# Stored gate vectors as 32 rows, a last norm of two operations per half, and a residual rebuilt by the next block

## The chip, the cores and the metric

The kernel runs on one core of a Trainium2 chip. The engines of the core are named as in the profile: PE (TensorE, matmuls) with its weight loads as PEld, DVE (VectorE), ACT (ScalarE), POOL (GpSimd) and SP (SyncE, which issues most transfers). The metric is the device time of one execution in microseconds; the time given is the median of several runs. An engine works through its own instructions in the order in which they were written to it, and waits on semaphores for what the others have to deliver.

## The reference

Two layers, each of three blocks: a feed-forward network, a mixer, a feed-forward network. Activations are 512 tokens of 1,024 float32 values. A conditioning vector gives shift, scale and gate for each block.

```
mod = (silu(c) @ ada_w[l] + ada_b[l]).reshape(Bn, N_SUB, 3, D_MODEL)
shift, scale, gate = mod[:, :, 0, None], mod[:, :, 1, None], mod[:, :, 2, None]
h = x * (1.0 + scale[:, 0]) + shift[:, 0]
y = swiglu(h, ffn_w1[l, 0], ffn_w3[l, 0], ffn_w2[l, 0])
x = layer_norm(ALPHA * x + 0.5 * (1.0 + gate[:, 0]) * y, ln_g[l, 0], ln_b[l, 0])
```

`swiglu(h, w1, w3, w2)` is `(silu(h @ w1) * (h @ w3)) @ w2` with an inner width of 2,816. The second block has `hybrid_mixer` (attention, spatial gating and a state-space scan over one input and one output projection) in place of `swiglu` and a weight of 1 in place of 0.5, and the third is like the first. The result is x after the third block of the second layer.

## The kernel before

All float32 matmuls are three matmuls of a reduced format, on a high and a low part of each operand (`mm3`, L121 to L123). Weights come in tiles of 128x1024 (512 KB) by SP's queue into four buffers `raw`; `wsplit` has ACT make the high part (L103) and DVE the low part (L105). `wsplit_s` does so in halves, named wsh and wsl (L116, L117), for the last four tiles of w2 in an FFN.

**An FFN** (`ffn`) first projects two lead tiles of the inner width (four in the first block), then the others one by one: tiles h of w1 and w3 over 1,024 inputs, `swiglu`, and the result split into `ghi` and `glo`. After each half of the 22 tiles come the down matmuls y. The gate is no operation on y: `down_weights` multiplies each w2 tile by the row G on DVE (L101, L111) before it is split. In the second half the last four w2 tiles are kept, and the matmuls go token block by token block (four blocks of 128 tokens, numbered 0 to 3; 24 matmuls each), so that the norm of one block runs beside the matmuls of the next.

**The norm** (`post_norm`). DVE adds y to the residual x in two halves (L242) with statistics behind each (L243), aggregates them (L256) and prepares the variance (L230); POOL raises it to the power -0.5 (L231); DVE makes the second scale factor (L258); ACT writes the normed block z (L267), not yet multiplied by ln_g and ln_b. `flush` calls `spread`: PE transposes z into PSUM (hps, L213), ACT and DVE apply the next block's scale and shift to it (hsum, L224 and L222), and it is split into `hT_hi` and `hT_lo` (L226, L227), the operands of the next block. What the next block needs of x itself, the residual, is z times ln_g plus ln_b: `renew` writes it with two 128x1024 DVE operations per token block (L279, L280), called at the end of `ffn` and of `mixer`. z, lg, lb and G share a pool of eight buffers of 128x1024 (`big`) with the background work's tiles.

In the last block there is no next one: ACT writes z in halves, DVE multiplies and adds (L263, L264), and each half is stored to the output. For token blocks 0 to 2 the statistics there are a sum taken with the addition (L239) and a sum of squares on ACT.

**The gate vectors.** `ada_vec` computes one of the 18 vectors of 1,024 values as 128x8 (value 128k+p in partition p, column k). It runs in the background of the other work, a step at a time (`make_bg`). A gate (j == 2) has to become a row that is the same in all partitions, so it is stored to DRAM by POOL's queue (L183) and read back by `gate_par` with a broadcast (L188):

```
G.dma_start(bass.AP(tensor=d.tensor, offset=d.offset, ap=[[1, 128], [128, 8]]), acc)
load(g, bcast_row(mods[l, s, 2][0], 1024))
```

**The order.** Each engine's order follows from the order in which the program is written and from a scheduler in the tile framework. `tc.issue_after(ins)` puts what is written inside it behind the instruction `ins` on that instruction's engine. The mixer begins with two groups of matmuls per token block, tA (24 of 128x284) and tB (24 of 128x256), in the same PSUM pool as part of the FFN's y; a GELU on DVE reads tB.

Five changes from one block to the next are spoken of by letters: A (first FFN to first mixer, near 380 us), B (mixer to FFN, near 680), C (FFN to the next layer's FFN, near 1,050), D (FFN to second mixer, near 1,410), E (mixer to last FFN, near 1,710). The last FFN's end is the tail.

## Time and profile before

| | us |
|---|---|
| median of 3 runs (2077.01 to 2079.93) | 2077.14 |
| the profiled execution's own time | 2078.03 |
| its span in the profile | 2076.3 |
| PE busy | 2036.6 |
| DVE busy | 1325.9 |
| ACT busy | 771.7 |
| POOL busy | 33.4 |

The mean granted clock of PE is 0.996 of full speed. The profile gives times of instructions in microseconds from the start of the span. "Busy" is time in which an engine had an instruction in work; where two overlap, it counts once. An idle time in square brackets stands before an instruction, with what ended it. "PEclk" is the granted clock of a stretch: 1.00 is the 2.4 GHz level, 0.50 the 1.2 GHz level. A transfer's landing is the time from its issue to its end.

### The profile page before, as it was taken

How to read it: one execution, taken by the hardware profiler on the slowest of the kernel's cores; microseconds unless marked ns; L12 is line 12 of the kernel's file. 1: busy time of each engine (PE TensorE's matmuls, PEld its weight loads, DVE VectorE, ACT ScalarE, POOL GpSimd, SP SyncE). 2: the span in 40 equal slices, each digit the busy share in tenths (PEclk: the TensorE clock that was granted, in tenths of full speed). 3: DMA queues.
4: the chain of work that ended last, by engine and by line, in shares of the span. 5: the costliest groups of instructions: out<-in, count | busy, mean ns of one | idle time of the engine just before them, and what ended most of it. 6: DMA issues, size and time to landing. Idle time of an engine off the chain costs nothing.

```text
span 2076.3 us, 25861 instructions
## 1 busy us (share of the span) xinstructions
PE 2036.6 (98%) x9992; PEld 1650.7 (79%) x9992; DVE 1325.9 (64%) x2423; ACT 771.7 (37%) x1350; POOL 33.4 (2%) x49
## 2 busy tenths in 40 slices
PE   7999999999999999999999999999999999999997
PEld 6888887887666988888888888888776678888886
DVE  6756437778898647444754644478788984354354
ACT  4422223525556422222442222235356573222222
POOL 0000000000000000000000000000000000000000
PEclk9999999999999999999999999999999999999999
DMA  8765425224452544432644443252254523232321
GB/s 334 258 177 209 168 88 157 91 97 166 133 164 90 183 142 151 143 123 83 177 125 132 144 152 126 86 145 102 92 173 132 171 79 128 71 122 94 99 92 41
DMA packets 84599, 282.34 MB, mean 136 GB/s; under 512 B 13267, under 2 KB 13523, under 8 KB 84476
## 3 DMA queue, kind: packets, MB, share of 16 engines
q1 hardware_dynamic: 83612, 278.02, 41.3%
q0 software_dynamic: 864, 2.67, 0.4%
q8 instruction: 78, 1.28, 0.2%
q14 instruction: 45, 0.37, 0.1%
HBM read 278.51 MB, written 4.76 MB: 136 GB/s over the span
## 4 chain that ended last, share of the span: by engine, by line
PE 88%; DVE 6%; DMA 2%; ACT 2%; issue 1%; POOL 0%; SPq 0%; POOLq 0%; ACTq 0%; DVEq 0%
PE h L121 15%; PE h L122 15%; PE h L123 15%; PE y L121 7%; PE y L123 7%; PE y L122 7%; PE pj L121 3%; PE pj L122 3%; PE pj L123 3%; PE op L925 3%; PE tp L915 2%; DMA raw<-in_w_dram 1%; PE S L884 1%; DVE wlo L105 1%; PE S L885 1%
## 5 line engine op out<-in xcount | busy, mean ns | idle before, releaser
L103 ACT CAST whi<-raw 128x1024 fp32r<-128x1024 f32 x308 | 320.5, 1047 | 748.0 <-issue 393.6
L121 PE MATMUL h<-hT_hi,whi 128*128 128x512 f32 (+1 forms) x1504 | 565.3, 377 | 12.9 <-ACT hT_hi L1059 12.9
L122 PE MATMUL h<-hT_lo,whi 128*128 128x512 f32 (+1 forms) x1504 | 565.9, 376 | 0.0
L123 PE MATMUL h<-hT_hi,wlo 128*128 128x512 f32 (+1 forms) x1504 | 565.5, 376 | 0.0
L105 DVE TENSOR_TENSOR wlo<-raw,whi 128x1024 fp32r<-128x1024 f32 x308 | 372.7, 1215 | 263.9 <-ACT whi L103 263.4
L121 PEld LDWEIGHTS h<-hT_hi,whi 128*128 128x128 f32 x1504 | 283.5, 189 | 64.3 <-ACT hT_hi L1059 12.9
L122 PEld LDWEIGHTS h<-hT_lo,whi 128*128 128x128 f32 x1504 | 283.6, 189 | 51.5 <-DVE hT_lo L1060 0.4
L123 PEld LDWEIGHTS h<-hT_hi,wlo 128*128 128x128 f32 x1504 | 283.6, 189 | 51.4
L121 PE MATMUL y<-whi,ghi 128*128 128x512 f32 x576 | 224.1, 389 | 0.0
L122 PE MATMUL y<-wlo,ghi 128*128 128x512 f32 x576 | 224.1, 389 | 0.0
L123 PE MATMUL y<-whi,glo 128*128 128x512 f32 x576 | 224.1, 389 | 0.0
L311 DVE TENSOR_TENSOR th<-th,h 128x512 f32<-128x512 f32 x88 | 60.4, 687 | 226.7 <-PE h L123 226.0
L154 DVE CUSTOM_DVE_ANT_0 raw<-raw,csil 128x1024 f32<-128x1024 f32 x144 | 174.2, 1217 | 0.9 <-DMA raw<-in_ada_w_dram 0.8
L123 PEld LDWEIGHTS y<-whi,glo 128*128 128x128 f32 x576 | 108.1, 188 | 22.5
L121 PEld LDWEIGHTS y<-whi,ghi 128*128 128x128 f32 x576 | 108.1, 188 | 22.4
L122 PEld LDWEIGHTS y<-wlo,ghi 128*128 128x128 f32 x576 | 108.1, 188 | 22.4
L121 PE MATMUL pj<-hT_hi,whi 128*128 128x512 f32 x288 | 117.4, 408 | 0.0
L122 PE MATMUL pj<-hT_lo,whi 128*128 128x512 f32 x288 | 113.7, 395 | 0.0
L123 PE MATMUL pj<-hT_hi,wlo 128*128 128x512 f32 x288 | 113.3, 393 | 0.0
L101 DVE TENSOR_TENSOR raw<-raw,G 128x1024 f32<-128x1024 f32 x86 | 104.3, 1218 | 4.0 <-DMA raw<-in_w_dram 4.0
L314 ACT CAST ghi<-th 128x512 fp32r<-128x512 f32 x88 | 54.4, 618 | 136.1 <-DVE th L311 136.1
L917 ACT COPY pt<-tp 128x512 f32<-128x512 f32 (+2 forms) x96 | 54.8, 584 | 83.9 <-PE tp L915 82.8
(284 smaller groups left out, 2528.1 us busy)
## 6 DMA issues: line engine op xcount, KB each, us to landing
raw<-in_w_dram SPq DMA_DIRECT2D x256, 512.0 KB, 3.6
raw<-in_ada_w_dram SPq DMA_DIRECT2D x144, 512.0 KB, 4.4
raw<-in_wS_dram SPq DMA_DIRECT2D x36, 512.0 KB, 3.6
raw<-in_cw_dram SPq DMA_DIRECT2D x16, 512.0 KB, 3.8
raw<-in_wo_dram SPq DMA_DIRECT2D x16, 512.0 KB, 4.5
raw<-in_wl_dram SPq DMA_DIRECT2D x8, 512.0 KB, 9.0
T<-lane SPq DMA_DIRECT2D x16, 256.0 KB, 3.7
G<-mod SPq DMA_DIRECT2D x6, 512.0 KB, 6.1
```

Of the source, the lines that this page charges most:

```text
L101: V.tensor_mul(raw, raw, gain)
L103: S.copy(hi[:, :n], raw[:, :n])
L105: V.tensor_sub(lo[:, :n], raw[:, :n], hi[:, :n].bitcast(F32))
L121: PE.matmul(o, lh, rh, start=first, stop=False)
L122: PE.matmul(o, lh, rl, start=False, stop=False)
L123: PE.matmul(o, ll, rh, start=False, stop=last)
L154: V.tensor_tensor_reduce(out=raw, in0=raw, in1=cond["c"], scale=0.5, scalar=0.0, op0=ALU.mult, op1=ALU.add, accum_out=acc[:, k:k + 1])
L311: freed[0] = V.tensor_mul(th, th, h3).ins
L314: S.copy(hi, th)
L915: PE.transpose(tp[0:n, e * 128:(e + 1) * 128], pr[e][:, kb * 128:kb * 128 + n], ident)
L917: S.copy(pt[0:n, :], tp[0:n, :])
L925: PE.matmul(op[r, :], v, pt[0:n, g * 256:(g + 1) * 256], start=(br == 0), stop=(br == 2 and kb == qb))
```

## The change

Three parts. First, the gate vector is put together in the first 8 columns of a raw buffer, DVE transposes 32x32 squares of it, and what was 128x8 becomes four groups of 8 rows of 32 values, each stored by a DMA of its own; G is read back by POOL's queue and no longer by SP's. Second, in the last block z becomes (x - mean)*ln_g, written before the power is known, and the output z*power + ln_b (`finish`); both are DVE operations, and the finish of token block 2 is held until behind the aggregation of block 3. Third, `renew` is called by the following block and stands behind the last scale factor of the norm.

```diff
-        else:
+        elif j == 1:
             V.scalar_tensor_tensor(acc, acc, 1.0, ab, op0=ALU.add, op1=ALU.add)
         mods[l, s, j] = acc
         if j == 2:
+            V.scalar_tensor_tensor(raw[:, 0:8], acc, 1.0, ab, op0=ALU.add, op1=ALU.add)
+            V.transpose(raw[:, 32:64], raw[:, 0:32])
             d = dram.tile([1, 1024], F32, tag=nm("mod"), name=nm("mod"))
-            G.dma_start(bass.AP(tensor=d.tensor, offset=d.offset, ap=[[1, 128], [128, 8]]), acc)
+            for b in range(4):
+                G.dma_start(bass.AP(tensor=d.tensor, offset=d.offset + 32 * b, ap=[[128, 8], [1, 32]]),
+                            raw[32 * b:32 * b + 8, 32:64])
             mods[l, s, j] = d
...
-        load(g, bcast_row(mods[l, s, 2][0], 1024))
+        G.dma_start(g, bcast_row(mods[l, s, 2][0], 1024))
...
+    def finish(b, mv, P):
+        for q in range(2):
+            sl = slice(q * 512, (q + 1) * 512)
+            x = x_sb[:, b, sl]
+            V.scalar_tensor_tensor(x, P["t"][b][:, sl], mv[:, 2:3], P["lb"][:, sl], op0=ALU.mult, op1=ALU.add)
+            load(out[b * 128:(b + 1) * 128, sl], x)
...
-            V.tensor_mul(mv[:, 3:4], mv[:, 0:1], mv[:, 2:3])
...
-            V.scalar_tensor_tensor(mv[:, 3:4], mv[:, 0:1], -1.0, mv[:, 2:3], op0=ALU.mult, op1=ALU.mult)
+            if not last:
+                P["moved"] = V.scalar_tensor_tensor(mv[:, 3:4], mv[:, 0:1], -1.0, mv[:, 2:3], op0=ALU.mult,
+                                                    op1=ALU.mult).ins
         if last:
+            P.setdefault("t", {})[b] = z
             for q in range(2):
                 sl = slice(q * 512, (q + 1) * 512)
-                S.activation(z[:, sl], x[:, sl], AF.Identity, bias=mv[:, 3:4], scale=mv[:, 2:3])
-                V.tensor_mul(x[:, sl], z[:, sl], P["lg"][:, sl])
-                V.tensor_add(x[:, sl], x[:, sl], P["lb"][:, sl])
-                load(out[b * 128:(b + 1) * 128, sl], x[:, sl])
+                V.scalar_tensor_tensor(z[:, sl], x[:, sl], mv[:, 0:1], P["lg"][:, sl],
+                                       op0=ALU.add if b < 3 else ALU.subtract, op1=ALU.mult)
+            if b == 2:
+                P["held"] = mv
+            elif b == 3:
+                with tc.issue_after(aggr.ins):
+                    finish(2, P["held"], P)
+                finish(b, mv, P)
+            else:
+                finish(b, mv, P)
             return
...
     def renew(P, n=0):
-        while len(P.get("zz", [])) > n:
-            x, z = P["zz"].pop(0)
-            V.tensor_mul(x, z, P["lg"])
-            V.tensor_add(x, x, P["lb"])
+        if len(P.get("zz", [])) > n:
+            with tc.issue_after(P["moved"]):
+                while len(P["zz"]) > n:
+                    x, z = P["zz"].pop(0)
+                    V.tensor_mul(x, z, P["lg"])
+                    V.tensor_add(x, x, P["lb"])
...
                 ahead = up_weights(todo[0])
+                catch_up()
...
         flush(P)
-        renew(P)
...
             V.bn_aggr(gmv[:, b * 2:b * 2 + 2], st)
+        catch_up()
...
+        catch_up = partial(renew, P)
         P = {}
```

The lines of the changed program carry other numbers: the addition is L247, the statistics L248, the aggregation L267, the preparation of the variance L235, the scale factor L270, the renewal L301 and L302, hT_lo L232, the transposes L218, and the matmuls L122 to L124.

How the order moves is shown at three places. The first is DVE at A, around the norm of token block 2 (statistics st_2698, mv_2699; the residual add of its halves reads y_2288 and y_2289). In the kernel before, renewals (L279, L280) of token block 1 stand between the additions and the aggregation:

```order
L242 TENSOR_TENSOR x_sb<-y_2288,x_sb 128x512
L279 TENSOR_TENSOR x_sb<-z_2640,lg_1093 128x1024
L227 TENSOR_TENSOR hT_lo<-hsum_2631,hT_hi 128x512
L243 BN_STATS st_2698<-x_sb 128x6
L242 TENSOR_TENSOR x_sb<-y_2289,x_sb 128x512
L280 TENSOR_TENSOR x_sb<-x_sb,lb_1094 128x1024
L243 BN_STATS st_2698<-x_sb 128x6
L227 TENSOR_TENSOR hT_lo<-hsum_2684,hT_hi 128x512
L222 TENSOR_SCALAR hsum_2691<-hps_2679,GA_1749,BB_1750 128x128
L256 BN_AGGR mv_2699<-st_2698 128x2
```

In the changed kernel the same token block (st_2706, mv_2707, y_2292 and y_2293) has no renewal there:

```order
L247 TENSOR_TENSOR x_sb<-y_2292,x_sb 128x512
L248 BN_STATS st_2706<-x_sb 128x6
L232 TENSOR_TENSOR hT_lo<-hsum_2639,hT_hi 128x512
L247 TENSOR_TENSOR x_sb<-y_2293,x_sb 128x512
L248 BN_STATS st_2706<-x_sb 128x6
L267 BN_AGGR mv_2707<-st_2706 128x2
L235 TENSOR_SCALAR mv_2707<-mv_2707 128x1
L270 SCALAR_TENSOR_TENSOR mv_2707<-mv_2707 128x1
```

All four renewals there now stand behind the last scale factor (mv_2767), among the first operations of the mixer (dtx):

```order
L270 SCALAR_TENSOR_TENSOR mv_2767<-mv_2767 128x1
L301 TENSOR_TENSOR x_sb<-z_2588,lg_1097 128x1024
L232 TENSOR_TENSOR hT_lo<-hsum_2752,hT_hi 128x512
L227 TENSOR_SCALAR hsum_2759<-hps_2747,GA_1753,BB_1754 128x128
L302 TENSOR_TENSOR x_sb<-x_sb,lb_1098 128x1024
L232 TENSOR_TENSOR hT_lo<-hsum_2759,hT_hi 128x512
L486 TENSOR_TENSOR dtx_2841<-tA_2848,p_461_2804 128x4
L301 TENSOR_TENSOR x_sb<-z_2648,lg_1097 128x1024
L301 TENSOR_TENSOR x_sb<-z_2708,lg_1097 128x1024
```

The operations are the same in number; what moved is the place of 128x1024 operations.

The second place is PE at A, from the last matmul y on. Before, nine matmuls tA stand between it and the transposes of token block 2 (z_2700):

```order
L123 MATMUL y_2291<-wsh_2547,glo_2267 128x512
L121 MATMUL tA_2848<-whi_2813,hT_hi 128x284
L122 MATMUL tA_2848<-wlo_2815,hT_hi 128x284
L123 MATMUL tA_2848<-whi_2813,hT_lo 128x284
...
L213 MATMUL hps_2734<-cst,z_2700 128x128 x4
L213 MATMUL hps_2739<-cst,z_2700 128x128 x4
```

In the changed kernel the transposes of that token block (z_2708) come directly behind the last y:

```order
L124 MATMUL y_2295<-wsh_2555,glo_2271 128x512
L218 MATMUL hps_2742<-cst,z_2708 128x128 x4
L218 MATMUL hps_2747<-cst,z_2708 128x128 x4
L122 MATMUL tA_2848<-whi_2813,hT_hi 128x284
L123 MATMUL tA_2848<-wlo_2815,hT_hi 128x284
```

The nine tA matmuls moved behind them; the transposes of token block 3 (z_2768) follow after 30 matmuls tA and tB.

The third place is DVE in the tail (st_16471 and mv_16472 are those of token block 3, z_16431 is block 2's). Before:

```order
L263 TENSOR_TENSOR x_sb<-z_16431,lg_14300 128x512
L242 TENSOR_TENSOR x_sb<-y_16080,x_sb 128x512
L264 TENSOR_TENSOR x_sb<-x_sb,lb_14301 128x512
L263 TENSOR_TENSOR x_sb<-z_16431,lg_14300 128x512
L243 BN_STATS st_16471<-x_sb 128x6
L264 TENSOR_TENSOR x_sb<-x_sb,lb_14301 128x512
L256 BN_AGGR mv_16472<-st_16471 128x2
```

Now (st_16482, mv_16483 and z_16484 are block 3's, z_16449 is block 2's):

```order
L247 TENSOR_TENSOR x_sb<-y_16104,x_sb 128x512
L248 BN_STATS st_16482<-x_sb 128x6
L267 BN_AGGR mv_16483<-st_16482 128x2
L254 SCALAR_TENSOR_TENSOR x_sb<-z_16449,mv_16448,lb_14325 128x512
L235 TENSOR_SCALAR mv_16483<-mv_16483 128x1
L276 SCALAR_TENSOR_TENSOR z_16484<-x_sb,mv_16483,lg_14324 128x512 x2
L254 SCALAR_TENSOR_TENSOR x_sb<-z_16449,mv_16448,lb_14325 128x512
L254 SCALAR_TENSOR_TENSOR x_sb<-z_16484,mv_16483,lb_14325 128x512 x2
```

Block 2's last operations moved behind the aggregation of block 3, and ACT has none of it.

## Rows read from the trace of the kernel before

**Rows 1.** The page's first part: busy time of each engine, its share of the span, and its instructions.

```profile
PE 2036.6 (98%) x9992; PEld 1650.7 (79%) x9992; DVE 1325.9 (64%) x2423; ACT 771.7 (37%) x1350; POOL 33.4 (2%) x49
```

**Rows 2.** The table of waits over the whole span, two of PE's: what waited, for what, us in total, times, the longest.

```profile
PE h L121 <- ACT hT_hi L1059: 12.9, 1, 12.9
...
PE hps L213 <- ACT z L267: 6.3, 5, 2.1
```

**Rows 3.** Busy time by stretch: the stretch in us and its length, then busy time (and instructions) of PE, PEld, DVE, ACT and POOL, the granted clock PEclk, the busy share of the DMA engines, and GB/s.

```profile
340.00:400.00 60.00, 55.55 (x288) 47.64 (x287) 43.69 (x73) 30.75 (x66) 2.83 (x5) 0.94 0.47 122
362.76:366.16 3.40, 3.40 (x9) 2.67 (x9) 3.33 (x5) 0.00 (x0) 0.00 (x0) 0.50 0.86 282
386.65:390.05 3.40, 3.40 (x17) 3.40 (x16) 2.50 (x6) 3.40 (x9) 0.55 (x1) 0.50 0.02 5
660.00:690.00 30.00, 28.75 (x188) 23.60 (x187) 25.77 (x51) 21.49 (x48) 2.55 (x2) 1.00 0.36 118
1015.00:1060.00 45.00, 43.32 (x267) 38.51 (x266) 34.04 (x55) 24.28 (x47) 2.21 (x4) 1.00 0.47 158
1380.00:1430.00 50.00, 47.85 (x292) 42.60 (x291) 37.16 (x68) 27.70 (x65) 2.81 (x5) 1.00 0.34 111
2060.00:2077.00 17.00, 3.69 (x17) 2.72 (x15) 9.91 (x22) 4.28 (x6) 1.10 (x2) 0.68 0.25 93
```

**Rows 4.** The same view, same columns, before and during a store of a gate vector (first two), and during and behind another (last two).

```profile
334.00:338.00 4.00, 4.00 (x19) 3.34 (x18) 4.00 (x5) 1.99 (x2) 0.00 (x0) 1.00 0.42 144
343.00:349.00 6.00, 6.00 (x28) 4.95 (x28) 0.98 (x2) 1.14 (x2) 0.00 (x0) 1.00 0.74 49
997.00:1004.00 7.00, 7.00 (x33) 5.79 (x32) 3.83 (x5) 1.24 (x3) 0.00 (x0) 1.00 0.62 43
1004.00:1008.00 4.00, 4.00 (x19) 3.34 (x18) 2.19 (x3) 1.14 (x2) 0.00 (x0) 1.00 0.86 321
```

**Rows 5.** The page's last part, transfers by what they move: queue, operation, count, KB each, median us from issue to landing. The third is the store of a gate vector, the second the load of G.

```profile
raw<-in_w_dram SPq DMA_DIRECT2D x256, 512.0 KB, 3.6
...
G<-mod SPq DMA_DIRECT2D x6, 512.0 KB, 6.1
...
mod<-mod POOLq DMA_DIRECT2D x6, 4.0 KB, 10.1
```

**Rows 6.** The chain that ended last, in order of time, near 340 us: start, us, what.

```profile
339.40 10.51 DMA raw<-in_w_dram
```

**Rows 7.** PE's instructions in time at A: start, us, engine, line, operation, out<-in, shapes, and in brackets the idle time before it with what ended it. Matmuls overlap, so the distance of starts is what one takes.

```profile
360.67 0.50 PE L121 MATMUL y<-wsh,ghi 128*128 128x512 f32 x1 [1.58 <-ACT wsh L116]
362.00 0.50 PE L122 MATMUL y<-wsl,ghi 128*128 128x512 f32 x1 [0.84 <-DVE wsl L117]
...
382.27 0.39 PE L123 MATMUL y<-wsh,glo 128*128 128x512 f32 x1
...
383.54 0.29 PE L123 MATMUL tA<-whi,hT_lo 128*128 128x284 f32 x1
385.86 1.26 PE L213 MATMUL hps<-cst,z 128*128 128x128 f32 x8 [2.03 <-ACT z L267]
```

**Rows 8.** DVE's instructions in time at A, same columns: the second residual add and the scale factor of token block 0, a renewal, and the second residual add and the scale factor of token block 2.

```profile
365.21 0.67 DVE L242 TENSOR_TENSOR x_sb<-y,x_sb 128x512 f32<-128x512 f32 x1
...
367.73 0.16 DVE L258 SCALAR_TENSOR_TENSOR mv<-mv 128x1 f32<-128x1 f32 x1 [0.68 <-POOL mv L231]
...
376.19 1.21 DVE L279 TENSOR_TENSOR x_sb<-z,lg 128x1024 f32<-128x1024 f32 x1
...
378.53 0.67 DVE L242 TENSOR_TENSOR x_sb<-y,x_sb 128x512 f32<-128x512 f32 x1
...
383.95 0.58 DVE L258 SCALAR_TENSOR_TENSOR mv<-mv 128x1 f32<-128x1 f32 x1
```

**Rows 9.** Instructions in time in the tail, same columns: the first and the last of the 96 matmuls y that go by token blocks, and DVE's operations around and behind the last.

```profile
2041.76 0.39 PE L121 MATMUL y<-wsh,ghi 128*128 128x512 f32 x1
...
2061.45 0.68 DVE L242 TENSOR_TENSOR x_sb<-y,x_sb 128x512 f32<-128x512 f32 x1
2062.16 0.69 DVE L243 BATCH_NORM_STATS2 st<-x_sb 128x6 f32<-128x512 f32 x1
...
2063.30 0.39 PE L123 MATMUL y<-wsh,glo 128*128 128x512 f32 x1
...
2064.76 0.69 DVE L263 TENSOR_TENSOR x_sb<-z,lg 128x512 f32<-128x512 f32 x1 [0.94 <-ACT z L262]
2065.36 0.68 DVE L242 TENSOR_TENSOR x_sb<-y,x_sb 128x512 f32<-128x512 f32 x1
...
2072.57 0.69 DVE L264 TENSOR_TENSOR x_sb<-x_sb,lb 128x512 f32<-128x512 f32 x1
```

**Rows 10.** Two of POOL's powers and the DVE operation that ran at the first of them, same columns.

```profile
682.58 1.21 DVE L105 TENSOR_TENSOR wlo<-raw,whi 128x1024 fp32r<-128x1024 f32 x1
...
682.80 2.00 POOL L231 TENSOR_TENSOR mv<-mv,mhalf 128x1 f32<-128x1 f32 x1 [10.61 <-DVE mv L230]
...
2063.07 0.55 POOL L231 TENSOR_TENSOR mv<-mv,mhalf 128x1 f32<-128x1 f32 x1 [6.04 <-DVE mv L230]
```

**Rows 11.** Instructions grouped by line, the renewal's two operations: out<-in and shapes, count, busy us, mean ns of one, idle before them with what ended most of it.

```profile
L279 DVE TENSOR_TENSOR x_sb<-z,lg 128x1024 f32<-128x1024 f32 x20 | 24.4, 1221 | 6.9 <-ACT z L267 6.9
L280 DVE TENSOR_TENSOR x_sb<-x_sb,lb 128x1024 f32<-128x1024 f32 x20 | 24.3, 1213 | 0.1
```

More of the change, by code (lines that the diff above doesn't have):

```diff
@@ L2 @@
 from contextlib import ExitStack
+from functools import partial
 import numpy as np
@@ L293, in project, with ffn @@
             mm3(o, hi[:, sl], lo[:, sl], hT(hT_hi, b0, b1, k), hT(hT_lo, b0, b1, k), k == 0, k == 7)
-    def ffn(l, s, P, last, bg, lead_order, params, feed=None, freed=None):
+    def ffn(l, s, P, last, bg, lead_order, params, catch_up, feed=None, freed=None):
         e = s // 2
@@ L426, in gelu2, with mixer @@
         V.scalar_tensor_tensor(dst, t[:, :n], 1.0, src, op0=ALU.add, op1=ALU.mult)
-    def mixer(l, P, last, lane, bg, gate_params, norm_params):
+    def mixer(l, P, last, lane, bg, catch_up, gate_params, norm_params):
         p0, p1 = slab("p0"), slab("p1")
@@ L1019, in mixer @@
         flush(P)
-        renew(P)
     P0 = {"GA": tiny("GA", 8), "BB": tiny("BB", 8)}
@@ L1119, in make_bg @@
         return bg
+    P = {}
     for n, (l, s) in enumerate(subs):
         last = n == len(subs) - 1
+        catch_up = partial(renew, P)
         P = {}
@@ L1138 @@
             cond.clear()
-            mixer(l, P, last, lane, make_bg(n, P), lambda: gate_par(l, s, P), lambda: norm_par(l, s, P))
+            mixer(l, P, last, lane, make_bg(n, P), catch_up, lambda: gate_par(l, s, P), lambda: norm_par(l, s, P))
         else:
@@ L1145 @@
             ffn(l, s, P, last, make_bg(n, P, gated), (2, 0) if after_mixer and QORDER[0] == 3 else (0, 2), params,
-                feed if n == 0 else None, gated)
+                catch_up, feed if n == 0 else None, gated)
 def _constants():
```

2 lines of the change are left out of this document (1 added, 1 removed).

## Prediction

> **What bounds the kernel now.** I read the page's first part, then what TensorE (PE) waited for, then a table of stretches, and only then single instructions. PE is busy 2036.6 of 2076.3 us [rows 1], so the other engines matter only where PE stands still: 39.7 us in all. PE's own waits show the first of them, 12.9 us at the program's start, which the change does not touch [rows 2]. The rest lies in few places [rows 3]: an end of some 13 us (17 us of stretch, 3.69 busy), and short idle spells at the five changes from one block to the next. Idle there is stretch less busy time: 4.45 us at 340 to 400 (first FFN to first mixer, "A" below), 1.25 at 660 to 690 (mixer to FFN, "B"), 1.68 at 1015 to 1060 (FFN to FFN, "C"), 2.15 at 1380 to 1430 (FFN to mixer, "D"); the second mixer's end ("E") I take to be like B. At A there is a further loss that idle time does not show: the granted clock is 0.50, the 1.2 GHz level, over two stretches of 3.40 us, each begun just after PE had stood still [rows 3, 7]. Half speed for 6.8 us costs 3.4 us.
>
> **Part 1, the gate vectors.** The old store puts 1,024 single floats in DRAM, one 4-byte element per address step, six times. It takes 10.1 us to land for 4 KB where 512 KB of weights take 3.6 [rows 5]; and while it lasts, all other transfers crawl: 49 GB/s at 343 to 349 against 144 just before, and 43 at 997 to 1004 against 321 just after [rows 4]. The first of these reaches PE. A load of w2 took 10.51 us [rows 6], so the splits of the last w2 tiles came late, and PE stood 1.58 and 0.84 us for them [rows 7]. The new store has 32 pieces of 128 bytes in four DMAs. No row shows such a store. Its cost lies between nothing and the old one's; 32 pieces are a 32nd of the count, so I take near nothing, which gives back 1.58 + 0.84 us and the first half-clock stretch, 1.7 us: 4.1 us. The other five stores fall where PE has work in hand, and I give them no gain. The price is a 128x32 transpose on VectorE (DVE) per vector, not shown before, bounded by 0 and the 0.69 us of a sixteen times larger operation [rows 9]; six of them are at most 4 us of DVE time over the whole run, beside PE's work. The load of G goes from SP's queue to POOL's. SP loses a load that could hold up the weights queued behind it. On POOL the load stands behind the last power of the norm, and in the mixers ahead of the RMS norm's power: if its buffer were late, that power would be too. G itself is wanted only when the down weights are scaled, most of half an FFN later. I cost it at nothing; uncovered, it would cost one landing, 6.1 us at the median [rows 5].
>
> The Trainium skill (DMA: Bandwidth & Descriptors, Specifications) says that below 512 B a transfer becomes a read-modify-write. By that rule 128-byte rows are still in the slow class, piece by piece; the traced store agrees that 4-byte pieces are slow, and no run here shows 128. If the slowness went by class and not by count, the 4.1 us would stay lost; that is the first rival.
>
> **Part 2, the renewal.** Each block of 128 tokens has its residual rebuilt by two 128x1024 operations, 1.221 and 1.213 us, 20 times over the five changes [rows 11]; nothing is removed, 48.7 us of DVE work moves. At A three of the four renewals stood ahead of the last scale factors, now none does. The last y matmul of A starts at 382.27, and 96 of them follow each other at (2063.30 - 2041.76)/95 = 0.227 us, 5.44 us per token block [rows 7, 9]. So token block 2's sums were complete at about 377.1; its second residual add began at 378.53, behind a renewal, and its scale factors came at 383.95, 5.4 us after that add, where token block 0 needed 2.5 (365.21 to 367.73) [rows 8]. Without renewals between, the factors come at about 379.9, z some 1.5 us later at 381.3, before y ends: the transposes that PE waited 2.03 us for [rows 7] can start at once, and the new order puts them directly behind y. Token block 3 then becomes the late one: its z ends near y's end + 4 us, or + 5.2 if ScalarE is still at the casts of block 2, and its transposes stand after one block of transposes (1.26) and 24 to 33 short tA matmuls, of which nine went from 382.27 to 383.54, 0.14 each [rows 7]: + 4.6 to + 5.9. I leave 0.5 us of idle for that at A and 0.4 at C and D. Gains: A 2.03 - 0.5 + 1.7 for the second half-clock stretch = 3.2; C 1.68 - 0.4 = 1.3; D 2.15 - 0.4 = 1.75. At B and E renewals also leave the crowded end of the attention; I take the idle time, 1.25 each, 2.5 together, with ends at -2 (the scheduler has reshuffled small matmuls there) and +4.
>
> What is late next: four renewals, 9.7 us, now fall into the first 14 us of the next block, between the last hT_lo pieces and, in the mixers, the GELU that frees PSUM banks. In an FFN the first two h tiles cover it. In a mixer, PE wants the first tB bank back some 14.5 us after y's end, and GELU is done at + 14 (both by counting the new order's rows up to there at these durations, so estimates): no stall, but no slack either. Bounds 0 to 4.9 us (two renewals more than before) at A and at D.
>
> **Part 3, the last norm.** PE's last matmul starts at 2063.30 and ends 0.39 later; the residual add that needed it started only at 2065.36, because DVE waited in order for z of token block 2 (2064.76), and the last DVE operation began at 2072.57 [rows 9]. The new order: add, stats, the same, aggregate, with nothing between. From the add at 2063.72: stats 0.71 later (2061.45 to 2062.16), aggregate another 0.7, at 2065.2. Then one remaining operation of block 2 (0.6), the small scale, two (x - mean)*g, one more of block 2, and the two last, each 0.6 apart: the last one starts at 2068.4 and ends at 2069.1, against 2072.57 + 0.69 = 2073.26. That is 4.2 us. But POOL's power runs beside these operations. It took 2.00 us at 682.80, when DVE was in an L105 begun at 682.58, and 0.55 at 2063.07 [rows 10]. If POOL gets its turn only when the run of three DVE operations is over, the end waits 0.7 us more: I take 3.5.
>
> The Trainium skill (SBUF — State Buffer, "SBUF: two separate sides") says that a DVE operation with two SBUF inputs and a GpSimd operation reading SBUF exclude each other for the whole instruction. The 2.00 us row agrees. It speaks against the new pair, which has two SBUF tensors each; without it the sum would gain 0.7 us more.
>
> **The sum.** 4.1 + 3.2 + 1.3 + 1.75 + 2.5 + 3.5 = 16.4 us off the profiled execution, which took 2078.03 us (span 2076.3): 2061.6. It lay 0.9 above the median of 2077.14, so I predict 2060.7.
>
> **Rivals.**
> 1. The 128-byte store still chokes the loads. For: nothing traced shows that size; the rule above. Against: the count. Loss of the 4.1: 2064.8.
> 2. The moved renewals hold up the mixers: GELU late at A and D by 4.9 us each, and a half-clock stretch of 1.7 behind each, 13.2 us, leaving 3.2 of the gain: 2073.9, no change within the bound. For: DVE is busy 43.69 of 60 us at A [rows 3]. Against: before, two renewals already stood there and only hps waited.
> 3. Slower: the four z tiles, lg and lb stay in six of the eight large buffers until the renewals are done. SP issues in order, so loads of the next block's norm vectors wait for these buffers with weights behind them. The second pair of up weights is wanted about 25 us after y's end (192 matmuls of half width at 0.114, 21.8, and the transposes); a load takes 3.6 [rows 5] and its two splits, of the renewals' size, about 2.4, so this decides once the renewals end later than about + 19. If they dragged to + 25, each of five changes would lose some 6 us, 30 in all: 2060.7 + 30 = 2091.
> 4. The attention's end gains its upper bound at B and E, where DVE is busy 25.77 of 30 us [rows 3]: 3 us more each, 2054.7.
>
> **Chances.** Forecast 0.56 (2057 to 2064 with its own bounds), rival 1 0.17, rival 2 0.09, rival 3 0.06, rival 4 0.12. A measurement of this kernel tells about 0.2%, 4.2 us, from no change. Faster: forecast, rivals 1 and 4 and a third of rival 2, near 0.87; same 0.07; slower 0.06. The range holds the forecast, rivals 1 and 4, and the way towards rival 2: 2054 to 2071.
>
> **What would show it.** No stretch under 60 GB/s behind a store of a gate vector, and no PE wait for wsh or wsl near 360; PEclk 1.00 through A; hps waits on z below 1 us in sum where they were 6.3; DVE's three renewals gone from between the residual adds; last DVE operation about 5.4 us behind PE's last, not 9.6; POOL's last power near 2 us if the lock is real. Waits of tA or tB on DVE, or SP waiting long on L301/L302 renewals, would say that rival 2 or 3 holds; a w2 load near 10 us at 340 that rival 1 does.

## The result and the profile after

The changed kernel takes 2062.31 us (median of 4 runs, 2062.18 to 2062.94), the kernel before 2078.19 in runs beside it (4 runs, 2077.01 to 2079.93): 15.9 us less, ratio 0.9921, 95% interval 0.9909 to 0.9932. The forecast was 2060.7 in a range of 2054 to 2071. The two profiled executions took 2078.03 and 2062.94, spans 2076.3 and 2061.2: 15.1 us between them.

The first part of the page after, beside [rows 1]:

```profile
PE 2032.4 (99%) x9992; PEld 1648.3 (80%) x9992; DVE 1328.4 (64%) x2425; ACT 764.5 (37%) x1342; POOL 43.0 (2%) x73
```

PE does the same 9992 instructions. Its busy time fell by 4.2 us, most of it time at half clock that is gone, and its idle time from 39.7 to 28.8. A stretch around the store of the second gate vector, beside [rows 4], and the stretches that answer to [rows 3], shifted by what had been gained before each, in the same columns:

```profile
343.00:351.00 8.00, 8.00 (x37) 6.63 (x36) 6.62 (x9) 3.50 (x6) 0.00 (x0) 1.00 0.59 165
340.00:400.00 60.00, 59.91 (x353) 53.29 (x352) 46.95 (x81) 32.60 (x73) 4.92 (x9) 1.00 0.39 124
650.00:680.00 30.00, 28.15 (x174) 21.81 (x173) 22.49 (x57) 23.14 (x52) 1.67 (x3) 1.00 0.33 103
1005.00:1050.00 45.00, 44.98 (x271) 39.93 (x270) 33.68 (x54) 23.21 (x45) 2.81 (x5) 1.00 0.36 119
1370.00:1420.00 50.00, 49.97 (x308) 45.01 (x307) 36.21 (x68) 26.02 (x63) 3.02 (x5) 1.00 0.30 93
2050.00:2061.00 11.00, 2.54 (x12) 1.77 (x10) 8.04 (x14) 0.00 (x0) 1.83 (x2) 0.80 0.26 95
```

Behind the store the transfers run at 165 GB/s, where they fell to 49 in [rows 4]. At A, C and D the idle time is 0.09, 0.02 and 0.03 us where it was 4.45, 1.68 and 2.15, and no stretch at A has the half clock. At B it is 1.85 where it was 1.25: nothing was won there. One of PE's waits (what waited, for what, us in total, times, longest), beside [rows 2]:

```profile
PE hps L218 <- ACT z L287: 1.0, 2, 0.5
```

The 6.3 us of waits for z are 1.0 (in a second trace of the changed kernel, taken with the experiments, 1.8). At A, DVE's order can be seen at work for the last token block (start, us, instruction, idle before it and its releaser):

```profile
375.71 0.68 DVE L247 TENSOR_TENSOR x_sb<-y,x_sb 128x512 f32<-128x512 f32 x1
...
378.18 0.69 DVE L247 TENSOR_TENSOR x_sb<-y,x_sb 128x512 f32<-128x512 f32 x1 [0.46 <-PE y L124]
...
380.69 0.16 DVE L270 SCALAR_TENSOR_TENSOR mv<-mv 128x1 f32<-128x1 f32 x1 [0.67 <-POOL mv L236]
380.77 1.22 DVE L301 TENSOR_TENSOR x_sb<-z,lg 128x1024 f32<-128x1024 f32 x1
```

These are the additions of token block 3, which now wait for PE instead of for renewals, its scale factor 2.5 us after the second addition, and only then the first renewal. Token block 2's transposes start at once behind the last y:

```profile
377.75 0.39 PE L124 MATMUL y<-wsh,glo 128*128 128x512 f32 x1
377.98 1.03 PE L218 MATMUL hps<-cst,z 128*128 128x128 f32 x8
```

The tail, DVE and POOL in time, beside [rows 9] and [rows 10]. PE's last matmul starts at 2052.16:

```profile
2052.58 0.69 DVE L247 TENSOR_TENSOR x_sb<-y,x_sb 128x512 f32<-128x512 f32 x1
...
2054.03 0.21 DVE L267 BATCH_NORM_AGGREGATE mv<-st 128x2 f32<-128x12 f32 x1
...
2054.84 1.40 DVE L276 SCALAR_TENSOR_TENSOR z<-x_sb,mv,lg 128x512 f32<-128x512 f32 x2
2056.16 2.07 DVE L254 SCALAR_TENSOR_TENSOR x_sb<-z,mv,lb 128x512 f32<-128x512 f32 x3
```

```profile
2055.07 0.92 POOL L236 TENSOR_TENSOR mv<-mv,mhalf 128x1 f32<-128x1 f32 x1 [4.16 <-DVE mv L235]
```

DVE does not stand still from the aggregation on, and ends at 2058.23, 6.07 us behind the start of the last matmul; before it was 2073.26, 9.96 behind it. (x2 and x3 are operations in a row; the last of the three starts at 2057.49.)

Where the time came from is read by the start of the same matmul in two traces, after less before, taken at the places below and differenced from place to place. "New store alone" is the experiment of that name, whose trace is set against the changed kernel's in the same way. The last column does the same with the second trace of the changed kernel and shows what two traces of one kernel differ by. The rows begin ahead of A; from the program's start to there the three gain 0.3, 1.0 and 0.9 us, which no row has. What each loses to the changed kernel, in us:

| stretch | before | new store alone | changed kernel again |
|---|---|---|---|
| A, until the matmuls y that go by token blocks | 4.6 | 0.0 | 0.0 |
| A, from there into the mixer (395) | 3.7 | 1.7 | 0.4 |
| first mixer (to 648) | 0.1 | 0.8 | 0.6 |
| B | -0.9 | -0.2 | 0.0 |
| C | 1.9 | 1.3 | 0.1 |
| D | 2.5 | 1.8 | 0.3 |
| E | -0.5 | -0.1 | 0.0 |
| tail | 4.0 | 4.0 | 0.0 |

So 0.8 in the first mixer is little more than two traces of one kernel differ by.

### The profile page after: what moved, and what is told of

The parts are those of the page before. It is cut to its first block, busy times and chain, and to the rows that moved or that the text cites. A ratio compares the mean times of both kernels' runs of the same rounds, so it can differ in the third digit from the quotient of the medians.

```text
span 2061.2 us, 25919 instructions
## 1 busy us (share of the span) xinstructions
PE 2032.4 (99%) x9992; PEld 1648.3 (80%) x9992; DVE 1328.4 (64%) x2425; ACT 764.5 (37%) x1342; POOL 43.0 (2%) x73
## 4 chain that ended last, share of the span: by engine, by line
PE 93%; DVE 4%; ACT 1%; DMA 1%; issue 0%; POOL 0%; SPq 0%; DVEq 0%; POOLq 0%; ACTq 0%
PE h L122 15%; PE h L123 15%; PE h L124 15%; PE y L122 9%; PE y L124 9%; PE y L123 9%; PE pj L122 3%; PE pj L124 3%; PE pj L123 3%; PE op L948 2%; PE tp L938 2%; PE S L907 1%; PE S L908 1%; DVE raw L155 1%; PE hps L218 1%; PE hid L641 1%
## 5 line engine op out<-in xcount | busy, mean ns | idle before, releaser
L122 PE MATMUL h<-hT_hi,whi 128*128 128x512 f32 (+1 forms) x1504 | 565.8, 377 | 12.8 <-ACT hT_hi L1081 12.8
L124 PE MATMUL h<-hT_hi,wlo 128*128 128x512 f32 (+1 forms) x1504 | 566.1, 376 | 0.0
L122 PEld LDWEIGHTS h<-hT_hi,whi 128*128 128x128 f32 x1504 | 283.7, 189 | 63.8 <-ACT hT_hi L1081 12.8
L124 PEld LDWEIGHTS h<-hT_hi,wlo 128*128 128x128 f32 x1504 | 283.9, 189 | 51.5
L124 PE MATMUL y<-whi,glo 128*128 128x512 f32 x576 | 224.2, 389 | 0.0
L122 PE MATMUL y<-whi,ghi 128*128 128x512 f32 x576 | 224.2, 389 | 0.0
L124 PEld LDWEIGHTS y<-whi,glo 128*128 128x128 f32 x576 | 108.2, 188 | 22.5
L122 PEld LDWEIGHTS y<-whi,ghi 128*128 128x128 f32 x576 | 108.2, 188 | 22.3
L122 PE MATMUL pj<-hT_hi,whi 128*128 128x512 f32 x288 | 117.4, 408 | 0.0
L124 PE MATMUL pj<-hT_hi,wlo 128*128 128x512 f32 x288 | 113.4, 394 | 0.0
L332 DVE SCALAR_TENSOR_TENSOR th<-th,h 128x512 f32<-128x512 f32 x88 | 60.0, 682 | 38.1 <-ACT th L331 38.1
```

The costliest lines, as they stand in the source:

```text
L122: PE.matmul(o, lh, rh, start=first, stop=False)
L124: PE.matmul(o, ll, rh, start=False, stop=last)
L332: V.scalar_tensor_tensor(th, th, 1.0, h1, op0=ALU.add, op1=ALU.mult)
```

## The experiments

All but one are edits of the changed kernel. They were timed in three later sets of runs, each on another chip, beside which the kernel before took 2083.5, 2082.5 and 2083.2 in the median. The changed kernel was run again in the third set alone, with the new store alone, the old renewals in the mixers with G on SP's queue, and the second kernel of pieces; the other experiments are compared with it across chips, so that differences near 1 us say little.

**The changed kernel again**, no edit.

> The changed kernel itself once more, as the base for the runs beside it. Kernels with the new store took about 2062 to 2065 us on both chips so far, the kernel before 2078 on one and 2083 on the other. Theory: the price of the old store differs from run to run and chip to chip (its loads wait behind a store that takes more or less long), the rest does not: 2062 to 2064 here, a gain of 16 to 21 us by what the kernel before takes on this chip. Rival: the chip itself is slower or faster, and both kernels move by the same per cent.

2062.59 (4 runs, 2062.27 to 2063.04); before 2083.20 (9 runs, 2080.76 to 2087.72); ratio 0.9899, interval 0.9886 to 0.9913. The changed kernel moved by 0.3 us between the two sets of runs, the kernel before by 5. So it is something in the kernel before that varies, as the theory has it, and the gain is 16 to 21 us; that both kernels move by the same per cent is ruled out. Experiments below are compared with 2062.59.

**The new store alone**, an edit of the kernel before:

```diff
+            V.scalar_tensor_tensor(raw[:, 0:8], acc, 1.0, ab, op0=ALU.add, op1=ALU.add)
+            V.transpose(raw[:, 32:64], raw[:, 0:32])
...
-            G.dma_start(bass.AP(tensor=d.tensor, offset=d.offset, ap=[[1, 128], [128, 8]]), acc)
+            for b in range(4):
+                G.dma_start(bass.AP(tensor=d.tensor, offset=d.offset + 32 * b, ap=[[128, 8], [1, 32]]),
+                            raw[32 * b:32 * b + 8, 32:64])
```

> The kernel before with the new store of the gate vectors alone (G still read by SP's queue, renewals and last norm as before). Theory: 4.1 us (the forecast's term) to 9 us (what undoing it cost on the other chip) faster than the kernel before on the same chip; the PE waits near 360 us and the first half-clock stretch gone, all transfers over 60 GB/s behind the stores; and its runs lie within 2 us of each other where those of the kernel before spread over 3 to 6. Rival: it gains less than 2 us, and the loss belonged to the renewals and the store together.

2071.05 (5 runs, 2070.73 to 2071.67): 12.2 us less than before, ratio 0.9940, interval 0.9928 to 0.9953, and a spread of 0.9 us where the kernel before has 7.0. The gain is above both ends of the expectation, and the old store's price is most of what varied. The 8.5 us that are left between this kernel and the changed one agree with the table: 1.7, 1.3 and 1.8 at A, C and D, 4.0 in the tail, less 0.3 at B and E. Stretch A and PE's wait for z:

```profile
340.00:400.00 60.00, 58.47 (x342) 51.78 (x342) 45.85 (x80) 32.32 (x72) 3.94 (x8) 1.00 0.37 119
```

```profile
379.90 1.09 PE L217 MATMUL hps<-cst,z 128*128 128x128 f32 x8 [1.53 <-ACT z L271]
```

The renewals are in their old place and PE waits 1.53 us for z, but PEclk is 1.00: no half clock follows this wait.

**The old store alone back.**

```diff
-            V.scalar_tensor_tensor(raw[:, 0:8], acc, 1.0, ab, op0=ALU.add, op1=ALU.add)
-            V.transpose(raw[:, 32:64], raw[:, 0:32])
+            V.scalar_tensor_tensor(acc, acc, 1.0, ab, op0=ALU.add, op1=ALU.add)
...
-            for b in range(4):
-                G.dma_start(bass.AP(tensor=d.tensor, offset=d.offset + 32 * b, ap=[[128, 8], [1, 32]]),
-                            raw[32 * b:32 * b + 8, 32:64])
+            G.dma_start(bass.AP(tensor=d.tensor, offset=d.offset, ap=[[1, 128], [128, 8]]), acc)
```

> The changed kernel with the old store of the gate vector alone (1,024 single floats by one DMA; the load of G stays on POOL's queue). Theory: the store chokes the loads behind it, the w2 tiles of the first FFN come late again, PE stands 1.5 to 2.5 us near 350 to 362 us and gets the half clock for 3.4 us behind it: 4.1 us more than the changed kernel, near 2066.4. Transfers fall under 60 GB/s for some 7 us behind the store. Rival: it was not the store but DVE's order at that place that made the splits late: no PE wait there, within 1 us of the changed kernel.

2073.77 (5 runs, 2071.97 to 2074.91): 11.2 us more, near the 12.2 that the new store gives by itself, and far from 4.1. PE's waits near 360, and two stretches:

```profile
357.57 0.50 PE L123 MATMUL y<-wsl,ghi 128*128 128x512 f32 x1 [1.20 <-DVE wsl L118]
363.35 0.50 PE L122 MATMUL y<-wsh,ghi 128*128 128x512 f32 x1 [2.98 <-ACT wsh L117]
364.68 0.51 PE L123 MATMUL y<-wsl,ghi 128*128 128x512 f32 x1 [0.84 <-DVE wsl L118]
```

```profile
343.00:351.00 8.00, 8.00 (x37) 6.63 (x36) 0.70 (x2) 1.14 (x2) 0.00 (x0) 1.00 0.68 32
...
365.66:369.07 3.41, 3.41 (x10) 2.66 (x9) 3.34 (x5) 0.00 (x0) 0.00 (x0) 0.50 0.80 261
```

Transfers crawl at 32 GB/s for eight us where it was 49 for six in [rows 4], PE stands 5.0 us instead of 2.4, and the half clock follows. No second stretch of half clock does: with the renewals moved PE waits 0.74 us for z at 390.64, and PEclk is 1.00 from 380 to 400. By the same matmuls A loses 8.3 us in this trace; C loses 1.4 more, with 0.84 of idle for a late w2 split ahead of the matmul at 1021.65, behind the fourth store; and D 1.3, where PE waits 0.94 for z behind the fifth, whose part in that wait was not traced.

**Pieces of other sizes and places.** One more store of 1,024 pieces behind each of four gate vectors, output unused; in two kernels:

```diff
+            m = {(0, 1): 32, (0, 2): 128, (1, 0): 1, (1, 1): 8}.get((l, s), 0)
+            if m:
...
+                G.dma_start(bass.AP(tensor=e.tensor, offset=e.offset, ap=[[16 * m, 128], [2 * m, 8], [1, m]]),
+                            raw[:, 0:8 * m].rearrange("p (k c) -> p k c", c=m))
```

> The changed kernel with one more store of 1,024 pieces behind each of four gate vectors, its output not used: pieces of 128 bytes behind the second gate vector (first mixer, near 340 us), 512 bytes behind the third, 4 bytes behind the fourth and 32 bytes behind the fifth. Theory by count: each chokes the loads alike, some 7 us under 60 GB/s, whatever the piece's size up to 128 bytes, and about 3 to 6 us are lost at the first. Rival by class of size: the 512-byte store lets the loads run, the 128-byte, 32-byte and 4-byte ones choke them alike; by bytes: the smaller the piece, the less.

```diff
+            m, name, ap = {(0, 1): (1, "near", [[1, 128], [128, 8], [1, 1]]),
+                           (0, 2): (1, "far", [[1024, 128], [128, 8], [1, 1]]),
+                           (1, 0): (8, "near8", [[8, 128], [1024, 8], [1, 8]]),
+                           (1, 1): (32, "near32", [[32, 128], [4096, 8], [1, 32]])}.get((l, s), (0, "", []))
+            if m:
...
+                G.dma_start(bass.AP(tensor=e.tensor, offset=e.offset, ap=ap),
...
```

> The changed kernel with one more store of 1,024 pieces behind each of four gate vectors, output not used. near: 4 bytes in the old store's pattern (neighbours in DRAM come from neighbouring partitions, behind the second vector). far: 4 bytes, each 512 bytes from the next (behind the third). near8: 32 bytes in the old pattern (behind the fourth). near32: 128 bytes in the old pattern (behind the fifth). Theory: it is neighbouring pieces below 64 bytes that meet in the same piece of DRAM, so near takes 8 us or more to land and loads crawl behind it, as in the kernel before, and far, near32 take under 5 us and choke nothing. Rival, by size alone: near and far choke alike. Rival, by count: all four choke.

The transfers by what they move, KB and us from issue to landing, first kernel, then second:

```profile
probe<-raw POOLq DMA_DIRECT2D x1, 512.0 KB, 3.9
...
probe<-raw POOLq DMA_DIRECT2D x1, 128.0 KB, 3.5
probe<-raw POOLq DMA_DIRECT2D x1, 32.0 KB, 2.9
probe<-raw POOLq DMA_DIRECT2D x1, 4.0 KB, 6.6
```

```profile
near<-raw POOLq DMA_DIRECT2D x1, 128.0 KB, 3.1
near<-raw POOLq DMA_DIRECT2D x1, 32.0 KB, 3.6
near<-raw POOLq DMA_DIRECT2D x1, 4.0 KB, 11.9
far<-raw POOLq DMA_DIRECT2D x1, 4.0 KB, 3.2
```

All have 1,024 pieces, so 512 bytes (512 KB), 128, 32 and 4 bytes each. Only small neighbours are slow: 4-byte pieces whose neighbours in DRAM come from neighbouring partitions take 11.9 us, 4-byte pieces 8 bytes apart within a partition's run 6.6, and 4-byte pieces 512 bytes apart 3.2, no more than 128-byte ones. The limit of 64 bytes in the expectation does not hold: neighbours of 32 bytes land in 3.6. The probes stood behind different vectors, with more or less traffic beside them. For the far pieces, at 645.64, the kernel before has the old store at nearly the same place, 647.88; it landed in 9.3 us, and none of its six was quick:

```profile
DMA to landing us min/median/max: 8.6/10.1/11.0
```

At the same stretch, 343 to 351, the second kernel (the 4-byte neighbours) and the first (1,024 pieces of 128 bytes):

```profile
343.00:351.00 8.00, 8.00 (x37) 6.63 (x36) 1.33 (x3) 1.16 (x3) 0.00 (x0) 1.00 0.87 40
```

```profile
343.00:351.00 8.00, 8.00 (x37) 6.64 (x36) 6.66 (x9) 3.01 (x6) 0.08 (x1) 1.00 0.61 173
```

40 GB/s against 173, and PE stood 2.37 and 0.84 us near 360 in the kernel with the neighbours and not at all in the other. In one run each they took 2069.14 and 2064.73. The theory by count falls, the rival by size falls too; the theory of neighbours holds for 4-byte pieces, in one trace of each kernel. While the far pieces were written no weights were loaded, so whether they choke other loads was not seen; beside the pieces 8 bytes apart (986.68 to 993.30) the transfers ran at 161 GB/s.

**G read by SP's queue.**

```diff
-        G.dma_start(g, bcast_row(mods[l, s, 2][0], 1024))
+        load(g, bcast_row(mods[l, s, 2][0], 1024))
```

> The changed kernel with the load of G back on SP's queue. Theory: the queue of this load is worth nothing, since G is wanted only half an FFN later: within 1 us of the changed kernel. Rival: on SP it waits for the new store with the weights queued behind it, and part of the gain in the first FFN belongs to the queue: 2 to 6 us more, with a PE wait near 350 to 362 us or at a start of an FFN.

2063.89 (4 runs, 2062.43 to 2064.38), 1.3 us more, a little above the theory's 1, across chips. Its trace, of the fastest of these runs, loses nothing near 360 or at a start of an FFN, the rival's places, and 0.5 us in the first mixer; what the slower runs lost was not seen.

**The old renewals.** `renew(P)` again at the end of `ffn` and `mixer`:

```diff
-        if len(P.get("zz", [])) > n:
-            with tc.issue_after(P["moved"]):
-                while len(P["zz"]) > n:
...
+        while len(P.get("zz", [])) > n:
...
         flush(P)
+        renew(P)
...
         flush(P)
+        renew(P)
```

> The changed kernel with the renewals called at the end of each block as before. Theory, from the distance of the two traces at the same matmuls: at A 3.3, C 1.9, D 2.6 are lost, at B and E 0.4 each is won, 7.0 us more in sum, near 2069.3; PE waits 1.6 to 2.1 us for z at A, C and D, and at A the half clock follows. Rival, the forecast's own terms: 3.2 + 1.3 + 1.75 + 2.5 = 8.75 more, near 2071.1, with PE's idle time at B and E larger than in the changed kernel. Second rival: the store had cleared most of A already, and only 4 us more.

2070.34 (5 runs, 2068.26 to 2071.77), 7.8 us more, between theory and rival. The trace, of its fastest run, loses 6.3 us from the first matmul on: 1.6 at A, 1.7 each at C and D, and 1.4 at E, where PE waits 1.33 for hT_lo, a wait that the kernel before does not have. At A PE waits 1.48 for z, at full clock (PEclk 1.00 from 340 to 400). The next two runs take that apart.

**The old renewals in the mixers alone.**

```diff
         tick(99)
         flush(P)
+        while P["zz"]:
+            x, z = P["zz"].pop(0)
+            V.tensor_mul(x, z, P["lg"])
+            V.tensor_add(x, x, P["lb"])
```

> The changed kernel with the renewals of the two mixers alone (B and E) called at the mixer's end as before; A, C and D as changed. Theory: the renewals were not what PE waited for at the attention's end, so putting them back costs nothing: 0 to 1 us faster than the changed kernel, PE's idle time in the 30 us around B near 1.2 where the changed kernel has 1.85. Rival, the forecast's term: 2.5 us slower, since idle time at B and E belongs to the renewals.

2065.13 (4 runs, 2064.36 to 2065.77), 2.5 us more: the rival's number. But the place is another. B loses nothing in the trace (-0.2); E loses 1.8, all in one wait of PE, and DVE shows what it hangs on:

```profile
1707.83 0.39 PE L123 MATMUL h<-hT_lo,whi 128*128 128x256 f32 x1 [1.66 <-DVE hT_lo L232]
```

```profile
1706.48 0.69 DVE L195 TENSOR_SCALAR G<-G 128x1024 f32<-128x1024 f32 x1 [2.34 <-DMA G<-mod]
1707.09 0.68 DVE L232 TENSOR_TENSOR hT_lo<-hsum,hT_hi 128x512 fp32r<-128x512 f32 x1
```

DVE stands 2.34 us for G's load, since the scaling of G was put ahead of the last hT_lo.

**The same with G read by SP's queue.** Both edits together.

> The changed kernel with the renewals of the two mixers called at the mixer's end as before, and G read by SP's queue. Theory: the 1.7 us that PE lost near 1706 us with the mixers' renewals put back was a wait of DVE for G's load, which stood ahead of the last hT_lo; here G's scaling stands behind it, so that wait is gone and B and E together are 0.3 to 1 us faster than in the changed kernel: the renewals' move is worth nothing at the attention's end. Rival: the wait comes back, and the move is worth 1.5 us or more at E.

2063.32 (4 runs, 2063.05 to 2063.61), 0.7 us more. The scaling of G now stands behind hT_lo, the wait for hT_lo is gone, and by the same matmuls B and E are 0.2 and 0.1 us faster than in the changed kernel. So the renewals' move is worth nothing at B and E; the theory holds, its gain of 0.3 us or more is just not reached, and the 0.7 us of the runs is not seen in the trace.

**Every renewal twice.**

```diff
+                    for _ in range(2):
-                    V.tensor_mul(x, z, P["lg"])
-                    V.tensor_add(x, x, P["lb"])
+                        V.tensor_mul(x, z, P["lg"])
+                        V.tensor_add(x, x, P["lb"])
```

> The changed kernel with every renewal done twice (x = z*lg, x + lb, and both again), 9.7 us more of DVE work behind each change of block. Theory of the forecast: in the mixers there is no slack, GELU frees its PSUM bank just in time, so A and D lose most of the added work, 5 to 9 us each with a half-clock stretch behind, and the FFNs hide it: 2075 to 2083. Rival: the mixers have slack of their own, under 2 us more in all, near 2063; then the forecast's count of DVE's order there was too tight.

2075.12 (5 runs, 2072.87 to 2075.64), 12.5 us more. In the trace the FFNs lose nothing and the two mixers 6.5 and 4.9. PE's waits over the span, and the stretch behind the first of the two:

```profile
PE pj L122 <- DVE gv L449: 6.0, 2, 3.0
```

```profile
407.27:414.10 6.83, 6.14 (x14) 4.44 (x15) 5.91 (x10) 1.04 (x1) 1.93 (x1) 0.50 0.47 145
```

PE waits 3.0 us in each mixer for the last GELU, which frees a PSUM bank, and the half clock follows, 6.8 us of it in the first and 3.4 in the second. But the GELU is not what came late. PE and DVE here (the projection pj, L124 its matmul with a low part of the weights):

```profile
407.96 0.79 PE L122 MATMUL pj<-hT_hi,whi 128*128 128x512 f32 x1 [2.99 <-DVE gv L449]
...
409.09 0.79 PE L124 MATMUL pj<-hT_hi,wlo 128*128 128x512 f32 x1
```

```profile
407.49 0.42 DVE L449 SCALAR_TENSOR_TENSOR gv<-gl,tB 128x256 f32<-128x256 f32 x1
407.82 1.22 DVE L106 TENSOR_TENSOR wlo<-raw,whi 128x1024 fp32r<-128x1024 f32 x1
```

and DVE in the changed kernel, where PE does not wait:

```profile
400.48 1.23 DVE L106 TENSOR_TENSOR wlo<-raw,whi 128x1024 fp32r<-128x1024 f32 x1 [0.91 <-ACT whi L104]
...
407.79 0.41 DVE L448 SCALAR_TENSOR_TENSOR gv<-gl,tB 128x256 f32<-128x256 f32 x1
```

The last GELU starts 0.3 us earlier than in the changed kernel. What comes 7.3 us later is the first low part of the projection's weights, behind the doubled renewals. PE's order then begins three projections before the first matmul with a low part, and it is the third that needs the GELU's bank. Of 9.7 us added, PE stood 3.0.

**The old last norm** (ACT's z, multiplication and addition in place of `finish`):

```diff
-                V.scalar_tensor_tensor(z[:, sl], x[:, sl], mv[:, 0:1], P["lg"][:, sl],
-                                       op0=ALU.add if b < 3 else ALU.subtract, op1=ALU.mult)
...
+                S.activation(z[:, sl], x[:, sl], AF.Identity, bias=mv[:, 3:4], scale=mv[:, 2:3])
+                V.tensor_mul(x[:, sl], z[:, sl], P["lg"][:, sl])
+                V.tensor_add(x[:, sl], x[:, sl], P["lb"][:, sl])
...
```

> The changed kernel with the old last norm (ACT writes z, DVE multiplies and adds per half, nothing held). Theory: only the tail changes; the span ends 9.6 us after PE's last matmul's start where it was 5.6 and more in the changed kernel: 4.0 us more, near 2066.3. Rival, the forecast's term: 3.5 more. The traces tell them apart by the start of the last DVE operation against PE's last matmul.

2067.55 (4 runs, 2065.81 to 2069.20), 5.0 us more. In the trace the tail behind PE's last matmul is 3.9 us longer, and the last DVE operation starts 9.35 us behind it, where the changed kernel's starts 5.33 behind: the theory's 4.0. The profiled execution lost another 2.2 ahead of the tail, most of it in small waits at D and in the second mixer, which the edit does not touch.

**The finish not held.** `finish(b, mv, P)` at once for every token block.

```diff
-            if b == 2:
-                P["held"] = mv
-            elif b == 3:
-                with tc.issue_after(aggr.ins):
-                    finish(2, P["held"], P)
-                finish(b, mv, P)
-            else:
-                finish(b, mv, P)
+            finish(b, mv, P)
```

> The changed kernel with the two last operations of token block 2 not held behind the aggregation of block 3. Theory: DVE then stands for POOL's power of block 2 (about 1 us) and does two more 0.65 us operations ahead of the residual add of block 3, which comes some 1.5 to 2 us later; of this the operations are saved at the end: 0.5 to 1.5 us slower than the changed kernel. Rival: the scheduler finds the same order without the hold, no change.

2062.73 (4 runs, 2062.22 to 2063.37), 0.1 us more: the rival's number, but DVE's order did change, the finish of block 2 standing ahead of the additions:

```profile
2050.99 1.41 DVE L254 SCALAR_TENSOR_TENSOR x_sb<-z,mv,lb 128x512 f32<-128x512 f32 x2
2052.31 1.28 DVE L247 TENSOR_TENSOR x_sb<-y,x_sb 128x512 f32<-128x512 f32 x2
```

It did not stand for the power, and what it does early it need not do late. Neither expectation had that: the tail is bounded by the number of DVE's operations, in either order.

## Why the prediction came out

The total came out partly by luck: terms were wrong in opposite directions. In the profiled pair A gave 8.3 us for a forecast of 4.1 + 3.2, C and D 4.4 for 3.05 and the tail 4.0 for 3.5, together 2.9 more; B and E lost 1.4 where 2.5 were to be won, 3.9 less. And the time was right because it was set out from an execution of 2078: where the kernel before takes 2083, the same change takes off 20.6 us, not 16.4. From the table and the runs:

- **The store, forecast 4.1.** It was too small. In the profiled executions A gained 4.6 up to the y matmuls that go by token blocks, near the forecast (idle for the w2 splits and the first half-clock stretch). The second half-clock stretch of [rows 3], 1.7, stood only in the trace that had the old store and the old renewals both: with the new store alone PE still waits 1.53 us for z and keeps full clock, and with the old store and the moved renewals, where the wait for z is 0.74, no second stretch follows. So the 1.7 can be credited to either; the forecast gave it to the renewals. Why the wait of 2.03 us at A was followed by the half clock and the one of 2.09 at D (kernel before, 1410.85) was not, no run shows. Counted with the store, A gains 6.6 (before less new store alone). In the runs of the later set the store is worth 12.2. The step that failed was to take the price from one execution: the old store's duration differs from run to run (six us of crawl in one trace, eight in another). "The other five stores ... no gain" failed too, by the 1.4 us at C in the old store's run; in the profiled pair they cost 0.5 at C and 0.8 at D at most (before less new store alone).
- **128 bytes by count, and rival 1.** Near nothing was right: a new store's 1 KB DMAs land in 3.5 us at the median, and nothing crawls. The transpose, bounded by 0.69, takes 0.20. But count was the wrong reason, since 1,024 pieces of 128 bytes do not choke either. The Trainium skill (DMA: Bandwidth & Descriptors, Specifications) gives 512 bytes as the least transfer for full rate, with a read-modify-write below it. That makes no difference between the pieces below 512 bytes, and here the difference lies there: pieces of 32 and 128 bytes, and of 4 bytes 512 apart, land in 2.9 to 3.6 us, 4-byte neighbours in 11.9, and 512-byte ones in 3.9. Whether the quick ones are read-modify-writes no run shows.
- **Renewals at C and D, 1.3 and 1.75.** Measured with the new store alone against the changed kernel: 1.3 and 1.8. The step was right, but its size is partly luck: the waits for z were 1.10 and 1.61 there, and 1.65 and 2.09 in the kernel before from which the forecast took off 0.4. The 0.4 left for token block 3 did not show in the changed kernel's first trace (idle 0.02 and 0.03); in its second C and D lose 0.1 and 0.3.
- **Renewals at A, 3.2.** 1.7: the idle part, 1.53, came out, again as a shorter wait (1.53 for 2.03) with nothing left, where the forecast had left 0.5 (0.09 idle in the first trace, 0.44 in the second). The 1.7 of half clock is gone with the new store alone.
- **Renewals at B and E, 2.5.** Wrong: 0.3 lost in sum, against the new store alone. The step that failed was to take the idle time of a stretch for the renewals', because DVE is busy there. PE's idle at B by releaser, before and then after:

```profile
669.47 0.65 PE L925 MATMUL op<-pt,vW 128*64 128x256 f32 x4 [0.29 <-ACT pt L917]
671.15 0.50 PE L121 MATMUL y<-whi,hT_hi 128*128 128x512 f32 x1 [0.66 <-ACT hsum L224]
...
686.32 1.09 PE L213 MATMUL hps<-cst,z 128*128 128x128 f32 x8 [0.26 <-ACT z L267]
```

```profile
653.10 0.50 PE L122 MATMUL y<-whi,hT_hi 128*128 128x512 f32 x1 [0.35 <-DVE hsum L227]
662.40 0.66 PE L218 MATMUL hps<-cst,z 128*128 128x128 f32 x4 [0.35 <-DVE x_sb L247]
663.71 0.50 PE L122 MATMUL y<-whi,hT_hi 128*128 128x512 f32 x1 [0.65 <-ACT hsum L229]
...
676.74 1.09 PE L218 MATMUL hps<-cst,z 128*128 128x128 f32 x8 [0.49 <-ACT z L287]
```

  Only 0.3 of 1.2 us before was a wait for z. The rest was ACT's copy of the attention's probabilities and the y matmuls behind the transposes, which no renewal delays; the 0.66 is still there as 0.65, and the wait for z is 0.49. Rival 4, the same credit at its upper bound, falls with it.
- **The tail, 3.5.** 4.0. The price of 0.7 for POOL's turn was not paid: the power took 0.92 us and ended at 2055.99, within the second of the two (x - mean)*g, not behind the run of three. The Trainium skill (SBUF — State Buffer, "SBUF: two separate sides") says that whichever of the two operations starts first shuts the other out for its whole length, that is, for one operation. The new trace agrees: the power, 0.55 undisturbed, ended 0.41 behind the first of the pair (2055.58). The prediction read the 2.00 of [rows 10] as agreeing too, but there DVE had a second operation right behind L105:

```profile
683.71 0.68 DVE L227 TENSOR_TENSOR hT_lo<-hsum,hT_hi 128x512 fp32r<-128x512 f32 x1
```

  It ended at 684.39, and the power 0.41 later. So POOL was held by two operations in a row there and by one here. What tells the two cases apart was not tried.
- **Rival 2.** Not seen in the changed kernel, where the mixers' starts have no wait of PE for DVE's GELU. With the renewals doubled PE does wait for the GELU's bank, with the half clock behind, but since low parts of weights came late, not the GELU. "No slack" was too tight: of 9.7 us more, PE stood 3.0.
- **Rival 3.** Even doubled, the renewals cost the FFNs' starts nothing.

Of the signs named beforehand most came as said: no crawl, no wait for wsh or wsl, full clock at A, last DVE operation 5.33 behind PE's last (before, by [rows 9], it was 9.27, not 9.6). The waits for z, said to fall below 1 us, were 1.0 and, in the second trace, 1.8. POOL's last power near 2 us did not come.

## What to carry to other kernels

Before a stretch's idle time is credited to a change, split it by releaser: here 2.5 us were credited to an engine that was busy, and PE waited for another. A half-clock stretch is not to be credited only to the wait just ahead of it: here the one behind a wait of 2.03 us was gone when the store alone was changed, though a wait of 1.53 stayed, and it did not come when the store alone was put back. Where a small vector is turned from columns into a row through DRAM, let it leave in longer runs: 32-byte neighbours landed in 3.6 us, and runs of 128 bytes, for one DVE transpose and four DMAs in place of one, removed 12 us in one set of runs, and most of the spread between runs.

## What had not been expected of the hardware

The slowness of a store of 1,024 small pieces is neither by count nor by size alone: 4-byte pieces 512 bytes apart land in 3.2 us, 4-byte neighbours from neighbouring partitions in 11.9, with other transfers at 40 GB/s. The price of such a store is not constant either: the kernel before spread over 2.9 us in the first set of runs and 5.8 to 7.0 in the later ones, on other chips, and moved by 5 between them, and with the new store alone it spread over 0.9. Why the price varies stays open, since the later runs of the kernel before left no trace; and it is not all that varies: the changed kernel with the old renewals or the old last norm spread over 3.5 us with the new store. And a load moved to another queue can hurt through an operation that waits for it: DVE's scaling of G, put ahead of the last hT_lo by the scheduler, cost PE 1.66 us in one experiment and 1.33 in another, and 0 in the changed kernel itself, where it stands behind hT_lo and renewals.
